# Turning new activations by DMA instead of by TensorE at the stage boundaries of a two-layer encoder

## Chip, cores and metric

The kernel runs on one core of one Trainium2 chip. The metric is the time of one execution in microseconds (us). Five engines work side by side, each through its own list of instructions in order: TensorE (PE, matrix products), VectorE (DVE), ScalarE (ACT), GpSimd (POOL) and SyncE (SP). DMA transfers are started by instructions in an engine's list, run on their own, and report by a semaphore.

## The reference

512 tokens of 1024 values pass two layers of four stages each, every stage ending in a residual and a layer norm.

```python
for i in range(DEPTH):   # 2
    x = layer_norm(ALPHA * x + 0.5 * swiglu(x, ffn_w_in[i, 0], ffn_w_out[i, 0]), ...)   # f
    x = layer_norm(ALPHA * x + token_mix(x, mix_w_in[i], ..., mix_w_out[i]), ...)        # m
    x = layer_norm(ALPHA * x + 0.5 * swiglu(x, ffn_w_in[i, 1], ffn_w_out[i, 1]), ...)   # f
    ple = sigmoid(x @ ple_w_gate[i] + ple_b_gate[i]) * (p[i] @ ple_w_proj[i])           # p
    x = layer_norm(ALPHA * x + ple, ...)

def swiglu(x, w_in, w_out):          # w_in 1024 x 5632, w_out 2816 x 1024
    gate, up = split(x @ w_in, 2, axis=-1)
    return (silu(gate) * up) @ w_out
```

`token_mix` is a projection to heads of stick-breaking attention, of a chunked gated delta rule and of a short convolution, and an output projection. All is float32.

## The kernel before

**Number format.** Every float32 factor of a product is split into a float16 high part and a float16 rest, `hi` and `lo`; `mm3` (L254) makes a product of three float16 products (L256 hi·hi, L257 hi·lo, L258 lo·hi). Weights come in by SP's DMAs as float32 (`raw`, three buffers; `f` for quads) and are split by `split_part`: ACT makes `hi` (L139), DVE makes `lo` (L140).

**Tiles.** Tokens stand in four tiles `t` of 128. `x_tok` holds x in token order, tokens on partitions. A product wants x with the 1024 features on partitions: `xT`, as `hi` and `lo`. At the end of each stage the out projection `out_proj(t)` (PE `po`, DVE adds the residual, L472) and `layer_norm(t)` make new x tile by tile. There are seven boundaries between stages: f to m twice, m to f twice, f to p twice, p to f once. At each, four tiles are turned.

**The turn.** `layer_norm` only notes the tile in `pending`; a later `flush` calls `to_T`: eight 128×128 float32 transpositions on PE into two PSUM banks (L220, `ps_t`), ACT copies `hi` into `xT` (L223), DVE subtracts for `lo` (L224). Flushes stand between the tiles of `out_proj`, in the gate stage (`ple`) and in the mix, and for the last tile in the ffn behind the first projections of the other three tiles.

**The ffn.** Its first two columns of 128 (m = 0, 1) are plain products. Three accumulators (`ahead`: gate m = 0, up m = 0, gate m = 1) are run first over tokens 0 to 383 and then, when the last tile is there, over 384 to 511; the up projection m = 1 follows when a silu (L345) has freed an accumulator. All other columns go in units of two by a scheme of seven products on 2×2 blocks (`begin`, `step`), which needs sums of weight blocks (`load_quad`, L453) and four sums of blocks of x, `xS`: halves of the features of even and odd token tiles combined. Before, they are formed from the PSUM banks (`ts`, L232, L236, L238) and split by `put_sums` (L248, L249). The products of a unit are numbered 0 to 6; those with `sums(n)` read `xS`. The columns are done in four groups, each followed by an `out_proj` over all tiles.

**Order.** The program is recorded stage by stage and a scheduler sets each engine's list; `after(a, b)` adds an order by hand. The buffers of `t2` (six) are shared by most temporaries.

Of the kernel before, what the change touches and what calls it, by code (L numbers as in the profile page):

```python
# [17 lines left out]
P = 128  # L18
D = 1024
# [14 lines left out]
class Block:  # L34
    def __init__(self, ctx, tc, ins, out):
        self.tc, self.nc, self.ins, self.out = tc, tc.nc, ins, out
        nc = self.nc
        pool = lambda name, **k: ctx.enter_context(tc.tile_pool(name=name, **k))
        self.const = pool("const", bufs=1)
        self.act = pool("act", bufs=1)  # L40
        self.rawp = pool("rawp", bufs=3)
        self.w2 = pool("w2", bufs=4)
        self.tmp = pool("tmp", bufs=6)
        self.small = pool("small", bufs=4)
        self.dram = pool("dram", bufs=2, space=bass.MemoryType.DRAM)
        self.psa = pool("psa", bufs=2, space=PSUM)
        self.psb = pool("psb", bufs=3, space=PSUM)
        self.psc = pool("psc", bufs=3, space=PSUM)
        self.pending, self.block_sums, self.put = [], [], 0
        self.constants()  # L50
# [126 lines left out]
    def layer_norm(self, t, y, gb, last=False):  # L177

        nc = self.nc
        g, b = gb  # L180
        st = self.small.tile([P, 2, 6], F32, name="st")
        for h in range(2):
            nc.vector.bn_stats(st[:, h], y[:, h * 512 : (h + 1) * 512])
        mv = self.small.tile([P, 2], F32, name="mv")
        nc.vector.bn_aggr(mv, st.rearrange("p a b -> p (a b)"))
        rs = self.small.tile([P, 2], F32, name="rs")
        nc.vector.tensor_scalar(rs[:, 0:1], mv[:, 1:2], LN_EPS / ALPHA**2, None, op0=ALU.add)
        nc.gpsimd.tensor_tensor(rs[:, 1:2], rs[:, 0:1], self.mhalf[:, 0:1], op=ALU.pow)
        halves = [y[:, h * 512 : (h + 1) * 512] for h in range(2)]
        for h, yh in enumerate(halves):  # L190
            nc.vector.scalar_tensor_tensor(
                yh, yh, mv[:, 0:1], g[:, h * 512 : (h + 1) * 512], op0=ALU.subtract, op1=ALU.mult
            )
        for h, yh in enumerate(halves):
            nc.vector.scalar_tensor_tensor(
                yh, yh, rs[:, 1:2], b[:, h * 512 : (h + 1) * 512], op0=ALU.mult, op1=ALU.add
            )
            if last:
                nc.sync.dma_start(
                    self.out[t * P : (t + 1) * P, h * 512 : (h + 1) * 512], yh  # L200
                )
        if not last:
            self.pending.append((self.xT, t, y, self.next_sums))

# [5 lines left out]

    def to_T(self, xT, t, y, sums):


        nc = self.nc
        banks = []
        for h in range(2):
            ps = self.bank("ps_t", (P, 4, P))
            for k in range(4):
                c = h * 512 + k * P
                nc.tensor.transpose(ps[:, k], y[:, c : c + P], self.ident)  # L220
            hi, lo = (xT[:, q, 4 * h : 4 * h + 4, t * P : (t + 1) * P] for q in range(2))
# [3 lines left out]
            )  # L225
            banks.append(ps)
        if not sums:
            return
        if t % 2 == 0:
            self.even = [self.t2("ts", (P, 4, P)) for _ in range(2)]  # L230
            for b, ps in zip(self.even, banks):
                nc.scalar.activation(b, ps, AF.Copy)  # L232
        else:
            b11, b21 = self.even
            n1, n2 = (self.t2("ts", (P, 4, P)) for _ in range(2))
            nc.vector.tensor_tensor(n1, b11, banks[0], op=ALU.subtract)  # L236
            for t, a, b in ((n2, banks[1], n1), (b11, n2, b11), (b21, n2, b21)):
                nc.vector.scalar_tensor_tensor(t, a, -1.0, b, op0=ALU.mult, op1=ALU.subtract)  # L238
            self.block_sums.append((n1, n2, b11, b21))

    def put_sums(self, xS):

        for ts in self.block_sums:
            a = self.put % 2
            self.put += 1
            for n, t in enumerate(ts):
                hi, lo = (xS[:, q, n, :, a * P : (a + 1) * P] for q in range(2))
                self.nc.scalar.activation(hi, t, AF.Copy)  # L248
                self.nc.vector.tensor_tensor(lo, t, hi, op=ALU.subtract)  # L249
        self.block_sums = []  # L250


    def mm3(self, ps, a, b, first, last, **k):

        nc = self.nc
        nc.tensor.matmul(ps, a[0], b[0], start=first, stop=False, **k)  # L256
        nc.tensor.matmul(ps, a[0], b[1], start=False, stop=False, **k)  # L257
        nc.tensor.matmul(ps, a[1], b[0], start=False, stop=last, **k)  # L258

    def ffn(self, i, f, j, last=False):  # L260
# [7 lines left out]
        with ExitStack() as ctx:  # L268
# [21 lines left out]

            if self.start:
                wg, wu = self.load_start(w_in, xT)
# [3 lines left out]

            def project(ps, w, m, a, b):
                for k in range(KD):
                    self.mm3(
                        ps[:, a:b], [w[:, h, k, m * P : (m + 1) * P] for h in range(2)],  # L300
                        [xT[:, h, k, a:b] for h in range(2)], k == 0, k == KD - 1,
                    )


# [22 lines left out]
            ahead = [(self.acc("pg"), wg, 0), (self.acc("pu"), wu, 0), (self.bank2("pg"), wg, 1)]  # L327
            for args in ahead:
                project(*args, 0, 384)
            self.flush()  # L330
            self.put_sums(xS)
            for args in ahead:
                project(*args, 384, 512)
            for m in range(2):
                if m == 1:
                    self.put_sums(xS)
                ps = []
# [48 lines left out]
            def step(new, old):  # L386

                if old is not None:
                    product(old.A, old.w, 5, sums(3), False, True)
                if new is not None:  # L390
                    product(new.A, new.w, 2, sums(1), False, False)
                    nc.scalar.activation(half(new.sg, 1), new.A, AF.Copy)  # L392
                if old is not None:
# [7 lines left out]
                if new is not None:  # L401
                    C = self.acc("pC")[:, : 2 * P].rearrange("p (a c) -> p a c", a=2)
                    product(C, new.w, 1, quarter(1, 0), True, True)
                    nc.vector.tensor_tensor(half(new.sg, 0), C, half(new.sg, 0), op=ALU.add)
                    product(new.A, new.w, 6, sums(2), False, False)
                    new.up = self.t2("up", (P, 2, P))
                    nc.scalar.activation(new.up, new.A, AF.Copy)  # L407
                    nc.vector.tensor_tensor(new.up, new.B, new.up, op=ALU.add)

            for gi, (m0, m1) in enumerate(groups):  # L410
# [10 lines left out]
                for t in range(NT):  # L421
                    self.out_proj(
                        t, lambda q, m: hT[(m0 + m) // 2][:, q, m % 2], wo, m1 - m0,
                        0.5 * IWS / ALPHA,
                    )
                    self.flush()
                    if gi == len(groups) - 1:
                        self.layer_norm(t, x[:, t], gb, last)

    def load_quad(self, w_in, m):  # L430
# [20 lines left out]
        def rest():  # L451
            for to, a, b in ((6, 0, 4), (4, 4, 5), (2, 0, 4), (3, 1, 2)):
                nc.vector.tensor_tensor(f[:, to], f[:, a], f[:, b], op=ALU.add)  # L453
            split(slice(4, 7), slice(2, 4))
# [3 lines left out]

    def out_proj(self, t, aT, wo, n, scale):

        for h in range(2):
            po = self.acc("po")
            for m in range(n):
                self.mm3(
                    po,
                    [aT(q, m)[:, t * P : (t + 1) * P] for q in range(2)],
                    [wo[m // 2][:, q, m % 2, h * 512 : (h + 1) * 512] for q in range(2)],
                    m == 0,
                    m == n - 1,
                )  # L470
            xs = self.x[:, t, h * 512 : (h + 1) * 512]
            self.nc.vector.scalar_tensor_tensor(xs, po, scale, xs, op0=ALU.mult, op1=ALU.add)  # L472


    def ple(self, i, j, last=False):
        nc, ins, x, xT = self.nc, self.ins, self.x, self.xT
        self.xT = self.act.tile([P, 2, KD, S], F16, name="xT", tag="xT", bufs=2)
        with self.tc.tile_pool(name="ple", bufs=1, reuse_waits="tile") as pool, \
# [12 lines left out]
            for t in range(NT):  # L491
# [9 lines left out]
                if t == 0:  # L501
                    for c in range(2):
# [10 lines left out]
                        )  # L513
                self.flush()
                for h in range(2):
# [43 lines left out]
    def mix_body(self, i, j, last, pool):  # L559
# [42 lines left out]
        for t in range(NT):  # L602
            if t == 3:
                self.flush()
            ts = slice(t * P, (t + 1) * P)
# [503 lines left out]
        for t in range(NT):  # L1109
            self.out_proj(t, lambda q, m: mT[:, q, m], wo, KD, IWS / ALPHA)  # L1110
            self.flush()
            self.layer_norm(t, x[:, t], gb, last)
# [9 lines left out]
    def load_tile(self, xT, t):  # L1122
        self.nc.sync.dma_start(self.x[:, t], self.ins["x"][0, t * P : (t + 1) * P, :])
        self.pending.append((xT, t, self.x[:, t], True))

    def load_start(self, w_in, xT):
# [4 lines left out]
        for c in range(2):  # L1131
            cs = slice(c * P, (c + 1) * P)
            for raw, w, c0 in zip(raws, ws, (0, DFF)):
# [4 lines left out]
                for k in (slice(0, 4), slice(4, 8)):  # L1138
                    parts = self.split_part(w[:, 0, k, cs], w[:, 1, k, cs], raw[:, k, cs])
                    for later, earlier in zip(parts, self.turned):  # L1140
                        self.after(later, earlier)
            if c == 0:
                self.load_tile(xT, NT - 1)
        return ws

@with_exitstack
def encoder_block(ctx: ExitStack, tc: tile.TileContext, ins, out, stages="fmfp", layers=range(DEPTH)):
# [3 lines left out]
    for (i, j, s), following in zip(n, n[1:] + [None]):  # L1151
        last = following is None
        k.next_sums = not last and following[2] == "f"
        if s == "f":
# [27 lines left out]
```

## Time and profile before

| | us |
|---|---|
| median of three runs | 2005.02 (2003.77 to 2005.6) |
| the profiled execution: its time | 2003.89 |
| its span, first to last instruction | 2002.2 |
| TensorE busy | 1951.1 |
| VectorE busy | 1522.9 |
| ScalarE busy | 870.6 |
| GpSimd busy | 69.9 |

The clock granted to TensorE was 0.997 of full speed. A row of the timeline has start, duration, engine, line, operation, out<-in, and in brackets the idle time before it and what ended it. A row of a group has line, engine, operation and shapes, then busy us and mean ns, then idle time before it by releaser. Products on TensorE overlap: a row's duration is longer than the step from one to the next. "PE x <- ACT y: 5.8, 2, 5.2" reads: PE's x waited for ACT's y 5.8 us in all, twice, the longest 5.2. The boundaries of the first layer stand at about 329 to 360 us (f to m), 599 to 637 (m to f), 932 to 963 (f to p) and 976 to 1023 (p to f).

### The profile page before, as it was taken

The numbers are of one execution on the slowest core, as the hardware profiler recorded it, in microseconds if no ns is written. First come the engines' busy times: TensorE is split into PE (matmuls) and PEld (weight loads), VectorE is DVE, ScalarE is ACT, GpSimd is POOL, SyncE is SP. The second block draws the span as 40 slices with busy tenths as digits, with TensorE's granted clock in tenths as the row PEclk, the third lists the DMA queues.
The fourth block names the chain that finished last, engine by engine and source line by source line (L and its number), as shares of the span: only waits on it lengthen the run. The fifth ranks groups of instructions, "written<-read, shape, count | busy, mean of one in ns | idle before, by whom it ended". The sixth has DMA issues, their size and how long they took to land.

```text
span 2002.2 us, 33105 instructions
## 1 busy us (share of the span) xinstructions
PE 1951.1 (97%) x14058; PEld 1271.2 (63%) x14058; DVE 1522.9 (76%) x2347; ACT 870.6 (43%) x1295; POOL 69.9 (3%) x92
## 2 busy tenths in 40 slices
PE   7999999999999999999999999999999999999998
PEld 5677686545555686776467685854455466776853
DVE  7995866775579895958897867667756897967586
ACT  6453442554445353444364444424634364443430
POOL 1000000110000000000000000002000000000000
PEclk9999999999999999999999999999999999999999
DMA  7543320421253533334224333213222524333221
GB/s 216 194 118 106 106 86 1 127 59 38 71 187 95 157 108 106 106 106 142 111 84 128 106 112 92 72 43 90 53 85 70 184 92 141 106 106 85 95 74 43
DMA packets 245359, 205.15 MB, mean 102 GB/s; under 512 B 20846, under 2 KB 225500, under 8 KB 245212
## 3 DMA queue, kind: packets, MB, share of 16 engines
q1 hardware_dynamic: 245212, 203.05, 33.0%
q8 instruction: 110, 1.80, 0.4%
q14 instruction: 37, 0.30, 0.0%
HBM read 200.14 MB, written 2.88 MB: 101 GB/s over the span
## 4 chain that ended last, share of the span: by engine, by line
PE 73%; DVE 15%; ACT 7%; issue 2%; DMA 2%; SPq 1%; POOL 0%; DVEq 0%; ACTq 0%
PE po L258 7%; PE po L256 7%; PE po L257 7%; PE pA L256 6%; PE pA L258 6%; PE pA L257 6%; DVE w L140 3%; PE pB L258 3%; PE pB L257 3%; PE pB L256 3%; DVE wq L140 2%; ACT w L139 2%; ACT wq L139 2%; PE pC L256 1%; PE pC L258 1%
## 5 line engine op out<-in xcount | busy, mean ns | idle before, releaser
L140 DVE SCALAR_TENSOR_TENSOR wq<-f,wq 128x1024 f16<-128x1024 f32 (+1 forms) x240 | 334.2, 1396 | 19.1 <-ACT wq L139 15.9
L139 ACT ACTIVATE wq<-f 128x1024 f16<-128x1024 f32 (+1 forms) x240 | 279.5, 1191 | 126.1 <-PE pB L258 83.2
L139 ACT ACTIVATE w<-raw 128x1024 f16<-128x1024 f32 (+1 forms) x196 | 193.6, 1031 | 264.9 <-PE po L258 226.2
L256 PE MATMUL po<-w,hT 128*128 128x512 f16 x704 | 266.7, 379 | 3.1 <-ACT hT L286 0.9
L256 PE MATMUL pA<-xS,wq 128*128 128x256 f16 x960 | 261.6, 272 | 6.9 <-ACT up L407 5.3
L257 PE MATMUL po<-w,hT 128*128 128x512 f16 x704 | 266.5, 379 | 0.0
L258 PE MATMUL po<-w,hT 128*128 128x512 f16 x704 | 264.3, 379 | 1.9 <-DVE hT L287 1.9
L258 PE MATMUL pA<-xS,wq 128*128 128x256 f16 x960 | 261.6, 273 | 0.0
L257 PE MATMUL pA<-xS,wq 128*128 128x256 f16 x960 | 261.6, 273 | 0.0
L140 DVE SCALAR_TENSOR_TENSOR w<-raw,w 128x1024 f16<-128x1024 f32 (+1 forms) x196 | 229.5, 1194 | 37.3 <-ACT w L139 37.3
L257 PEld LDWEIGHTS <-wq 128*128 128x128 f16 x2240 | 219.1, 98 | 42.0 <-issue 11.9
L453 DVE TENSOR_TENSOR f<-f 128x512 f32<-128x512 f32 x320 | 218.6, 687 | 27.2 <-DMA f<-in_ffn_w_in 22.1
L256 PEld LDWEIGHTS <-wq 128*128 128x128 f16 x2240 | 219.1, 98 | 30.2
L258 PEld LDWEIGHTS <-wq 128*128 128x128 f16 x2240 | 219.1, 98 | 27.3
L472 DVE SCALAR_TENSOR_TENSOR x_tok<-po,x_tok 128x512 f32<-128x512 f32 x144 | 97.6, 686 | 82.3 <-PE po L258 82.1
L395 DVE TENSOR_TENSOR sg<-pB,sg 128x256 f32<-128x256 f32 x80 | 33.7, 422 | 117.6 <-PE pB L258 117.6
L256 PEld LDWEIGHTS <-hT 128*128 128x128 f16 x704 | 68.8, 98 | 84.7 <-ACT hT L286 9.4
L258 PEld LDWEIGHTS <-hT 128*128 128x128 f16 x704 | 68.0, 98 | 84.8 <-DVE hT L287 5.3
L257 PEld LDWEIGHTS <-hT 128*128 128x128 f16 x704 | 68.9, 98 | 76.8 <-issue 1.3
L392 ACT ACTIVATE sg<-pA 128x256 f32<-128x256 f32 x80 | 30.5, 382 | 194.5 <-PE pA L258 194.5
L257 PEld LDWEIGHTS <-w 128*128 128x128 f16 x640 | 62.6, 98 | 67.0 <-issue 19.4
L223 ACT ACTIVATE xT<-ps_t 128x512 f16<-128x512 f32 x64 | 35.4, 594 | 150.6 <-PE ps_t L220 150.4
(290 smaller groups left out, 3851.5 us busy)
## 6 DMA issues: line engine op xcount, KB each, us to landing
f<-in_ffn_w_in SPq DMA_DIRECT2D x160, 512.0 KB, 5.0
raw<-in_ffn_w_out SPq DMA_DIRECT2D x44, 1024.0 KB, 5.2
raw<-in_mix_w_in SPq DMA_DIRECT2D x28, 1024.0 KB, 5.6
raw<-in_mix_w_out SPq DMA_DIRECT2D x8, 1024.0 KB, 4.9
raw<-in_ple_w_gate SPq DMA_DIRECT2D x8, 1024.0 KB, 6.1
raw<-in_ffn_w_in SPq DMA_DIRECT2D x6, 1024.0 KB, 5.1
ln_gb<-in_ln_g SPq DMA_DIRECT2D x8, 512.0 KB, 3.6
ln_gb<-in_ln_b SPq DMA_DIRECT2D x8, 512.0 KB, 4.7
```

The source lines that it names most:

```text
L139: self.nc.scalar.activation(hi, raw, AF.Copy, scale=WS),
L140: self.nc.vector.scalar_tensor_tensor(lo, raw, WS, hi, op0=ALU.mult, op1=ALU.subtract),
L223: nc.scalar.activation(hi, ps, AF.Copy),
L256: nc.tensor.matmul(ps, a[0], b[0], start=first, stop=False, **k)
L257: nc.tensor.matmul(ps, a[0], b[1], start=False, stop=False, **k)
L258: nc.tensor.matmul(ps, a[1], b[0], start=False, stop=last, **k)
L392: nc.scalar.activation(half(new.sg, 1), new.A, AF.Copy)
L395: nc.vector.tensor_tensor(half(old.sg, 1), old.B, half(old.sg, 1), op=ALU.add)
L453: nc.vector.tensor_tensor(f[:, to], f[:, a], f[:, b], op=ALU.add)
L472: self.nc.vector.scalar_tensor_tensor(xs, po, scale, xs, op0=ALU.mult, op1=ALU.add)
```

## The change

1. `flush` and `to_T` stay for the opening alone (32 transpositions). At a boundary `layer_norm` ends with `turn`: in token order ACT copies `hi` and DVE subtracts `lo` into `t2` tiles ("turn"), and ACT starts a transposing DMA for each into `xT`. Tiles 0 to 2 take two DMAs of 128×1024, tile 3 four of 128×512: 70 over seven boundaries.
2. The token sums are formed by DVE from `x_tok`, split in token order and turned by eight DMAs of 128×1024 per ffn: 32. In all 102 transposing DMAs, all started by ACT.
3. `put_sums` is called for tokens 0 to 255 behind the projections of the first 384 tokens, and for the rest behind those of the last 128.
4. In the first unit of a group product 2 runs after the product C (`sixth`); `out_proj` of the first tile of a group runs all but the last column of both halves first (`late`).
5. In the opening the first projections run in a given order, and the last tile's transpositions and some DVE sums are ordered behind others.

```diff
         if not last:
-            self.pending.append((self.xT, t, y, self.next_sums))
+            self.turn(self.xT, t, y)
...
-        if t % 2 == 0:
-            self.even = [self.t2("ts", (P, 4, P)) for _ in range(2)]
-            for b, ps in zip(self.even, banks):
-                nc.scalar.activation(b, ps, AF.Copy)
...
+    def pair_T(self, out, y, n):
+        nc = self.nc
+        hi, lo = (self.t2("turn", (P, n), F16) for _ in range(2))
+        self.turned = (
+            nc.scalar.activation(hi, y, AF.Copy), nc.vector.tensor_tensor(lo, y, hi, op=ALU.subtract)
+        )
+        for q, v in enumerate((hi, lo)):
+            nc.scalar.dma_start_transpose(out(q), v)
+
+    def turn(self, xT, t, y):
+        n = 1024 if t < NT - 1 else 512
+        for c in range(0, D, n):
+            ks = slice(c // P, (c + n) // P)
+            self.pair_T(lambda q: xT[:, q, ks, t * P : (t + 1) * P], y[:, c : c + n], n)
+
+    def put_sums(self, xS, a):
+        nc = self.nc
+        b11, b21, b12, b22 = (self.x[:, 2 * a + t, 512 * h : 512 * h + 512] for t in range(2) for h in range(2))
+        one, two = (self.tmp4.tile([P, 2, 512], F32, name="ts", tag="ts") for _ in range(2))
+        first = nc.vector.tensor_tensor(one[:, 0], b11, b12, op=ALU.subtract)
+        if self.opening:
+            self.after(first, self.turned[1] if a else self.parts[1])
+        for to, p, m in ((one[:, 1], b22, one[:, 0]), (two[:, 0], one[:, 1], b11), (two[:, 1], one[:, 1], b21)):
+            nc.vector.scalar_tensor_tensor(to, p, -1.0, m, op0=ALU.mult, op1=ALU.subtract)
+        for n, ts in ((0, one), (2, two)):
+            self.pair_T(
+                lambda q: xS[:, q, n : n + 2].rearrange("p n k c -> p (n k) c")[:, :, a * P : (a + 1) * P],
+                ts.rearrange("p n c -> p (n c)"), 1024,
+            )
...
-            for args in ahead:
-                project(*args, 0, 384)
-            self.flush()
-            self.put_sums(xS)
+            self.opening = first
+            for n, args in enumerate(ahead):
+                done = project(*args, 0, 384, done if first and n else None)
+                if first and n == 0:
+                    self.behind = done
+                    self.flush()
+                    self.behind = None
+            self.put_sums(xS, 0)
             for args in ahead:
                 project(*args, 384, 512)
+            self.put_sums(xS, 1)
             for m in range(2):
-                if m == 1:
-                    self.put_sums(xS)
...
-                if new is not None:
-                    product(new.A, new.w, 2, sums(1), False, False)
-                    nc.scalar.activation(half(new.sg, 1), new.A, AF.Copy)
+                if new is not None and old is not None:
+                    sixth(new)
...
                     nc.vector.tensor_tensor(half(new.sg, 0), C, half(new.sg, 0), op=ALU.add)
+                    if old is None:
+                        sixth(new)
...
+        if late:
+            for h in range(2):
+                part(h, range(n - 1))
+        for h in range(2):
+            if late:
+                part(h, [n - 1])
```

How ACT's list changes at three places. First the m to f boundary of the first layer. Before (`wq_6279` the first unit's weights, `xS_5948` the sums, `sg` the silus of m = 0 and 1):

```order
L223 ACTIVATE xT_5633<-ps_t_6055 128x4x128
L139 ACTIVATE wq_6279<-f_6276 128x1024
L139 ACTIVATE wq_6279<-f_6276 128x1536
L248 ACTIVATE xS_5948<-ts_6062 128x4x128
L345 ACTIVATE sg_6156<-pg_5973 128x512
L139 ACTIVATE wq_6279<-f_6276 128x1024
L248 ACTIVATE xS_5948<-ts_6063 128x4x128
L248 ACTIVATE xS_5948<-ts_5930 128x4x128
L248 ACTIVATE xS_5948<-ts_5931 128x4x128
L345 ACTIVATE sg_6187<-pg_5975 128x512
```

Now (`turn_6095` and `turn_6096` are hi and lo of sums 0 and 1 of tokens 256 to 511, `turn_6101` and `turn_6102` those of sums 2 and 3, `w_7157` a tile of out weights):

```order
L236 DMA_TRANSPOSE xS_5899<-turn_6012 128x8x128
L233 ACTIVATE turn_6095<-ts_6089 128x1024
L140 ACTIVATE w_7157<-raw_7155 128x1024
L236 DMA_TRANSPOSE xS_5899<-turn_6095 128x8x128
L236 DMA_TRANSPOSE xS_5899<-turn_6096 128x8x128
L233 ACTIVATE turn_6101<-ts_6090 128x1024
L140 ACTIVATE wq_6230<-f_6227 128x1024
L236 DMA_TRANSPOSE xS_5899<-turn_6101 128x8x128
L236 DMA_TRANSPOSE xS_5899<-turn_6102 128x8x128
L362 ACTIVATE sg_6107<-pg_5924 128x512
L362 ACTIVATE sg_6138<-pg_5926 128x512
```

The silus moved behind all transpositions of the sums, and a split of out weights stands ahead of the last four; it waits for PE's last product of the `ahead` accumulators, whose weight buffer it takes over.

Second, the f to m boundary, ACT, before (`sbv` belongs to the mix's v projections, `pv`):

```order
L223 ACTIVATE xT_201<-ps_t_3488 128x4x128
L139 ACTIVATE w_3671<-raw_3669 128x1024
L139 ACTIVATE w_3755<-raw_3753 128x1024 x2
L611 ACTIVATE sbv_3545<-pv_3547 128x256
L611 ACTIVATE sbv_3545<-pv_3574 128x256
L223 ACTIVATE xT_201<-ps_t_3628 128x4x128
L611 ACTIVATE sbv_3545<-pv_3601 128x256
L223 ACTIVATE xT_201<-ps_t_3635 128x4x128
```

Now:

```order
L140 ACTIVATE w_3732<-raw_3730 128x1024 x2
L233 ACTIVATE turn_3486<-x_tok_143 128x512
L236 DMA_TRANSPOSE xT_190<-turn_3486 128x4x128
L233 ACTIVATE turn_3492<-x_tok_143 128x512
L236 DMA_TRANSPOSE xT_190<-turn_3487 128x4x128
L236 DMA_TRANSPOSE xT_190<-turn_3492 128x4x128
L643 ACTIVATE sbv_3536<-pv_3538 128x256
L643 ACTIVATE sbv_3536<-pv_3565 128x256
L140 ACTIVATE w_3920<-raw_3918 128x1024
L236 DMA_TRANSPOSE xT_190<-turn_3493 128x4x128
```

The last transposition, of tile 3's `lo` for features 512 to 1023, came to stand behind the split of a third weight tile, whose load waits for DVE to have split the first (`w_3648`).

Third, ACT in the opening, before:

```order
L139 ACTIVATE w_656<-raw_654 128x1024
L248 ACTIVATE xS_200<-ts_326 128x4x128
L139 ACTIVATE w_693<-raw_691 128x1024
L248 ACTIVATE xS_200<-ts_196 128x4x128
L248 ACTIVATE xS_200<-ts_197 128x4x128
L139 ACTIVATE w_693<-raw_691 128x1024
L345 ACT_TABLE_LOAD
L345 ACTIVATE sg_419<-pg_236 128x512
```

Now:

```order
L236 DMA_TRANSPOSE xS_189<-turn_327 128x8x128
L140 ACTIVATE w_696<-raw_694 128x1024
L233 ACTIVATE turn_410<-ts_404 128x1024
L140 ACTIVATE w_696<-raw_694 128x1024
L236 DMA_TRANSPOSE xS_189<-turn_410 128x8x128
L236 DMA_TRANSPOSE xS_189<-turn_411 128x8x128
L233 ACTIVATE turn_416<-ts_405 128x1024
L140 ACTIVATE wq_545<-f_542 128x1024
L236 DMA_TRANSPOSE xS_189<-turn_416 128x8x128
L236 DMA_TRANSPOSE xS_189<-turn_417 128x8x128
L362 ACT_TABLE_LOAD
L362 ACTIVATE sg_422<-pg_225 128x512
```

The first silu now stands behind all eight transpositions of the opening's sums.

More of the change, by code (lines that the diff above doesn't have):

```diff
@@ L43, in __init__ @@
         self.tmp = pool("tmp", bufs=6)
+        self.tmp4 = pool("tmp4", bufs=2)
         self.small = pool("small", bufs=4)
@@ L48, in __init__ @@
         self.psc = pool("psc", bufs=3, space=PSUM)
-        self.pending, self.block_sums, self.put = [], [], 0
+        self.pending, self.behind = [], None
         self.constants()
@@ L209, in flush, with to_T @@
         self.pending = []
-    def to_T(self, xT, t, y, sums):
+    def to_T(self, xT, t, y):
         nc = self.nc
-        banks = []
         for h in range(2):
@@ L219, in to_T @@
                 c = h * 512 + k * P
-                nc.tensor.transpose(ps[:, k], y[:, c : c + P], self.ident)
+                turn = nc.tensor.transpose(ps[:, k], y[:, c : c + P], self.ident)
+                if self.behind is not None:
+                    self.after(turn, self.behind)
             hi, lo = (xT[:, q, 4 * h : 4 * h + 4, t * P : (t + 1) * P] for q in range(2))
@@ L225, in to_T @@
             )
-            banks.append(ps)
-        if not sums:
-            return
-        if t % 2 == 0:
-            self.even = [self.t2("ts", (P, 4, P)) for _ in range(2)]
-            for b, ps in zip(self.even, banks):
-                nc.scalar.activation(b, ps, AF.Copy)
[L233 to L253, printed above, removed]
-        nc = self.nc
-        nc.tensor.matmul(ps, a[0], b[0], start=first, stop=False, **k)
+    def pair_T(self, out, y, n):
+        nc = self.nc
+        hi, lo = (self.t2("turn", (P, n), F16) for _ in range(2))
[4 more added lines that the diff above has]
+            nc.scalar.dma_start_transpose(out(q), v)
@@ L257, in mm3 @@
+    def mm3(self, ps, a, b, first, last, behind=None, **k):
+        nc = self.nc
+        begun = nc.tensor.matmul(ps, a[0], b[0], start=first, stop=False, **k)
+        if behind is not None:
+            self.after(begun, behind)
         nc.tensor.matmul(ps, a[0], b[1], start=False, stop=False, **k)
-        nc.tensor.matmul(ps, a[1], b[0], start=False, stop=last, **k)
+        return nc.tensor.matmul(ps, a[1], b[0], start=False, stop=last, **k)
     def ffn(self, i, f, j, last=False):
@@ L289, in ffn @@
             self.quads = 0
-            if self.start:
+            first = self.start
+            if first:
                 wg, wu = self.load_start(w_in, xT)
@@ L295, in ffn, with project @@
                 wu = self.load_cols(w_in, DFF, self.w2)
-            def project(ps, w, m, a, b):
+            def project(ps, w, m, a, b, behind=None):
                 for k in range(KD):
-                    self.mm3(
+                    done = self.mm3(
                         ps[:, a:b], [w[:, h, k, m * P : (m + 1) * P] for h in range(2)],
-                        [xT[:, h, k, a:b] for h in range(2)], k == 0, k == KD - 1,
+                        [xT[:, h, k, a:b] for h in range(2)], k == 0, k == KD - 1, behind,
                     )
+                return done
             loads, loaded = [], []
@@ L408, in step, with sixth @@
                     nc.vector.tensor_tensor(new.up, new.B, new.up, op=ALU.add)
+            def sixth(u):
+                product(u.A, u.w, 2, sums(1), False, False)
+                nc.scalar.activation(half(u.sg, 1), u.A, AF.Copy)
             for gi, (m0, m1) in enumerate(groups):
@@ L423, in ffn @@
                         t, lambda q, m: hT[(m0 + m) // 2][:, q, m % 2], wo, m1 - m0,
-                        0.5 * IWS / ALPHA,
+                        0.5 * IWS / ALPHA, late=t == 0,
                     )
-                    self.flush()
                     if gi == len(groups) - 1:
@@ L452, in rest @@
             for to, a, b in ((6, 0, 4), (4, 4, 5), (2, 0, 4), (3, 1, 2)):
-                nc.vector.tensor_tensor(f[:, to], f[:, a], f[:, b], op=ALU.add)
+                total = nc.vector.tensor_tensor(f[:, to], f[:, a], f[:, b], op=ALU.add)
+                if self.opening and self.quads < 4:
+                    self.after(total, self.turned[1])
             split(slice(4, 7), slice(2, 4))
@@ L457, in load_quad, with out_proj, part @@
         return w, rest
[L459 to L463, printed above, removed]
+    def out_proj(self, t, aT, wo, n, scale, late=False):
+        po = [self.acc("po"), self.acc("po")] if late else [None] * 2
+        def part(h, ms):
+            for m in ms:
                 self.mm3(
-                    po,
+                    po[h],
                     [aT(q, m)[:, t * P : (t + 1) * P] for q in range(2)],
@@ L470, in out_proj @@
                 )
+        if late:
[4 more added lines that the diff above has]
+                part(h, [n - 1])
+            else:
+                po[h] = self.acc("po")
+                part(h, range(n))
             xs = self.x[:, t, h * 512 : (h + 1) * 512]
-            self.nc.vector.scalar_tensor_tensor(xs, po, scale, xs, op0=ALU.mult, op1=ALU.add)
+            self.nc.vector.scalar_tensor_tensor(xs, po[h], scale, xs, op0=ALU.mult, op1=ALU.add)
     def ple(self, i, j, last=False):
@@ L513, in ple @@
                         )
-                self.flush()
                 for h in range(2):
@@ L602, in mix_body @@
         for t in range(NT):
-            if t == 3:
-                self.flush()
             ts = slice(t * P, (t + 1) * P)
@@ L1110, in mix_body @@
             self.out_proj(t, lambda q, m: mT[:, q, m], wo, KD, IWS / ALPHA)
-            self.flush()
             self.layer_norm(t, x[:, t], gb, last)
@@ L1123, in load_tile @@
         self.nc.sync.dma_start(self.x[:, t], self.ins["x"][0, t * P : (t + 1) * P, :])
-        self.pending.append((xT, t, self.x[:, t], True))
+        self.pending.append((xT, t, self.x[:, t]))
     def load_start(self, w_in, xT):
@@ L1142, in load_start @@
             if c == 0:
+                self.parts = parts
                 self.load_tile(xT, NT - 1)
@@ L1152, in encoder_block @@
         last = following is None
-        k.next_sums = not last and following[2] == "f"
         if s == "f":
```

## The prediction

> **What bounds the kernel now.** I read the page's busy shares first, then the chain that ended last.
>
> ```profile
> span 2002.2 us, 33105 instructions
> PE 1951.1 (97%) x14058; PEld 1271.2 (63%) x14058; DVE 1522.9 (76%) x2347; ACT 870.6 (43%) x1295; POOL 69.9 (3%) x92
> PE 73%; DVE 15%; ACT 7%; issue 2%; DMA 2%; SPq 1%; POOL 0%; DVEq 0%; ACTq 0%
> ```
>
> TensorE (PE) works 97% of the span, so a microsecond taken from its stream, or a microsecond for which it waits, is a microsecond of the kernel. The profiled execution took 2003.89 us, 1.7 more than its span; the median of the runs shown is 1.1 above it. The sum is made against 2003.9 and 1.1 is added at the end. A change under 0.2% (4 us) could not be told from none.
>
> The waits of PE come next (sum in us, times, longest).
>
> ```profile
> PE pu L256 <- ACT sg L345: 5.8, 2, 5.2
> PE pA L256 <- ACT up L407: 5.3, 11, 1.8
> PE po L258 <- DVE hT L287: 1.9, 2, 0.9
> PE ps_t L220 <- DVE x_tok L195: 1.1, 1, 1.1
> PE po L256 <- ACT hT L286: 0.9, 4, 0.3
> PE pg L256 <- ACT xT L223: 0.8, 2, 0.4
> PE po L256 <- DVE sg L404: 0.7, 1, 0.7
> PE pv L256 <- DVE w L140: 0.5, 2, 0.3
> PE pg L257 <- DVE xT L224: 0.4, 2, 0.2
> ```
>
> Boundary waits are small: 2.8 us together (1.1, 0.8, 0.5, 0.4). The present scheme therefore costs PE its transpositions and little else.
>
> **Removed from PE.** Two answers: the group of the transpositions, and PE's timeline where one flush stands between products of the mix's out projection (start, us, engine, line).
>
> ```profile
> L220 PE MATMUL ps_t<-ident,x_tok x256: 272/273/445, 4.6 to 1951.5; 128*128 128x128 f32 x128
> ...
> 596.64 0.38 PE L258 MATMUL po<-w,mT 128*128 128x512 f16 x1
> ...
> 599.23 0.38 PE L258 MATMUL po<-w,mT 128*128 128x512 f16 x1
> 599.45 1.04 PE L220 MATMUL ps_t<-ident,x_tok 128*128 128x128 f32 x8
> 600.32 0.38 PE L256 MATMUL po<-w,mT 128*128 128x512 f16 x1
> ```
>
> Matmuls overlap, so the duration of 273 ns is not the price. From 596.64 to 599.23 stand twelve steps of a 512-wide product, so one is 0.216. Across the flush the step is 600.32 − 599.23 = 1.09: a flush of eight costs 0.87. Of 256 transpositions 32 belong to the opening and stay; 224 / 8 = 28 flushes go: 28 × 0.87 = **−24.4**. The 2.8 of boundary waits go with them: **−2.8**. By the Trainium skill ("VectorE: DVE Perf Modes", the rules for kernel authors) one should turn 128×128 on TensorE where PSUM will do, and take the DMA's crossbar otherwise; its table gives 390 ns against 1309. This trace has 0.11 us a block on PE's path, which makes the rule stronger here, but neither figure says what the DMA's time costs PE; that hangs on the cover, below.
>
> **Product order and held-back last products** (`sixth`, `late`). They aim at waits of the third fence: up 5.3, hT 1.9 + 0.9, sg 0.7, together 8.8. The opening's 1.8 and the two pairs near 0.9 look movable; the 0.3 ones repeat at groups that hold no spare product. I take a little over half, **−5**; ends 0 and −8.8.
>
> **What a turn costs now.** A tile's turn is an ACT copy, a DVE difference, and two DMAs that ACT issues in its own order. The copies have rows (behind the bar: busy us, mean ns; the page's list of DMAs: KB each, median us to landing; the DMA queue's timeline: start, us); no DMA transposition does.
>
> ```profile
> L139 ACT ACTIVATE w<-raw 128x1024 f16<-128x1024 f32 (+1 forms) x196 | 193.6, 1031 | 264.9 <-PE po L258 226.2
> L140 DVE SCALAR_TENSOR_TENSOR w<-raw,w 128x1024 f16<-128x1024 f32 (+1 forms) x196 | 229.5, 1194 | 37.3 <-ACT w L139 37.3
> ...
> raw<-in_mix_w_in SPq DMA_DIRECT2D x28, 1024.0 KB, 5.6
> out<-x_tok SPq DMA_DIRECT2D x8, 256.0 KB, 2.0
> ...
> 633.86 0.37 SPq L439 DMA_DIRECT2D f<-in_ffn_w_in  x1
> 354.69 9.27 SPq L148 DMA_DIRECT2D raw<-in_mix_w_in  x4
> ```
>
> So 1.03 for the copy, 1.19 for the difference. Landing: the nearest row is the 256 KB store out of the same x tile, 2.0 (the same bytes, also from SBUF); ends 2.0 and 5.6. Issue: 0.37 when the queue is idle, 9.27 / 4 = 2.3 when four large loads stand in it; ACT's queue carries nothing else, so I take 0.4.
>
> **Where PE then waits.** PE keeps its order; each stall is the landing less the work that covers it.
>
> *Mix to ffn, twice.* Rows of DVE and PE at the first such boundary:
>
> ```profile
> 612.18 0.69 DVE L183 BATCH_NORM_STATS2 st<-x_tok 128x6 f32<-128x512 f32 x1
> 617.88 1.41 DVE L195 SCALAR_TENSOR_TENSOR x_tok<-x_tok,rs,ln_gb 128x512 f32<-128x512 f32 x2
> ...
> 623.33 0.32 PE L256 MATMUL pg<-xT,w 128*128 128x384 f16 x1 [0.38 <-ACT xT L223]
> 635.22 0.33 PE L258 MATMUL pg<-xT,w 128*128 128x384 f16 x1
> ...
> 636.94 0.27 PE L256 MATMUL pA<-xT,wq 128*128 128x256 f16 x1
> 637.05 0.27 PE L257 MATMUL pA<-xT,wq 128*128 128x256 f16 x1
> ```
>
> Tile 2: after its out projection DVE runs six half-row steps of 0.6 (residual, statistics, two of the token sums, two weight sums) and the norm's four passes (2.7, twice the L195 row's 1.41 less overlap), 6.3; copy 1.0, difference 1.2, issue 0.4, landing 2.0: 10.9. PE's next out projection covers 48 × 0.216 = 10.4. Stall 0.4. Tile 3 has 12 us of cover (623.33 to 635.22) and needs none. Then ACT's queue: a split of out weights (`w_7157`) waits for PE's last first-projection product; the transpositions of the second token half's sums stand behind it. Split 1.03, two issues 0.8, landing 2.0, less 12 products × 0.11 = 1.3 that PE still has: stall 2.5. Both: 2 × 2.9 = **+5.8**.
>
> *Ffn to mix, twice.* ACT's last transposition (`turn_3493`) now stands behind a split whose load needs a buffer that DVE empties 3.7 after the last out projection (residual and statistics 1.2, two splits of 1.2, a short one). Load 5.6, split 1.0, issue 0.4, landing 2.0: 12.7. PE reads it in the middle of the fourth v projection:
>
> ```profile
> 353.28 0.28 PE L256 MATMUL pv<-wvab,xT 128*128 128x264 f16 x1
> 353.39 0.28 PE L257 MATMUL pv<-wvab,xT 128*128 128x264 f16 x1
> ```
>
> 84 products × 0.112 = 9.4. Stall 3.3; 2 × 3.3 = **+6.6**. The lower end is 0, if the load is early.
>
> *Gate stage to ffn, once.* The last tile's turn ends at 9.7 (DVE: residual, three weight splits, norm) + two half differences 1.3 + issue 0.4 + landing 2.0 = 13.4; cover 12.0 + 0.7. With the same 2.5 at the sums: **+3.2**.
>
> *Ffn to gate stage.* Before, DVE reaches the gate 6.9 after the residual of the last tile, and ACT splits a late load:
>
> ```profile
> 950.69 0.68 DVE L472 SCALAR_TENSOR_TENSOR x_tok<-po,x_tok 128x512 f32<-128x512 f32 x1
> 957.59 0.68 DVE L518 SCALAR_TENSOR_TENSOR gate<-pgate,bg 128x512 f32<-128x512 f32 x1
> ...
> 959.95 2.00 ACT L139 ACTIVATE w<-raw 128x1024 f16<-128x1024 f32 x2 [1.01 <-DMA raw<-in_ffn_w_out]
> ```
>
> Now five halves of weight splits and three turn differences stand ahead of the gate: 13.7 after the out projection, or 17 if the last tile's copy waits behind that late split; PE needs the accumulator that the gate frees at 48 × 0.216 = 10.4. I take **+4** (ends 0 and 6.7). The second time no ffn follows and none of these splits are there: 0.
>
> *Opening.* ACT reaches the first silu 7.3 after the out weights land:
>
> ```profile
> 26.78 1.06 ACT L139 ACTIVATE w<-raw 128x1024 f16<-128x1024 f32 x1 [4.58 <-DMA raw<-in_ffn_w_out]
> 32.77 1.28 ACT L345 ACT_TABLE_LOAD   x1
> 34.06 0.60 ACT L345 ACTIVATE sg<-pg 128x512 f32<-128x512 f32 x1
> ```
>
> The up projection waits for it (5.2, third fence). In the new order eight issues (3.2), three more 1024-wide copies (3.1) and a wait for the DVE sums stand between; I count it through to 41.1 for the silu's start, 7.1 later. PE has 17 products × 0.11 = 1.9 to put there: **+5.2**; ends 0 and 10.
>
> **Sum.** −24.4 − 2.8 − 5 + 5.8 + 6.6 + 3.2 + 4 + 5.2 = −7.4: 1996.5 for such an execution, 1997.6 with the 1.1; **1998**.
>
> **Rivals.**
> 1. *Hidden anyway.* All boundary transpositions land in time and only the opening's 5.2 stays: −24.4 − 2.8 − 5 + 5.2 = −27, 1978. For it: stalls are 0.4 to 3.3, small against covers of 9 to 12, and DVE loses the PSUM sums. Against it: the split ahead of the sums waits for PE itself, whatever lands when. Chance 0.25.
> 2. *ACT's issue time* (the other side). About 28 issues lie on the paths above (8 mix to ffn, 2 ffn to mix, 6 gate to ffn, 4 ffn to gate, 8 opening). Each 0.1 us of issue is 2.8 us; the gain is gone at 0.4 + 7.4 / 28 = 0.66, and at 1.4, inside the 2.3 row, the time is 1997.6 + 28 = 2026. Against it is the 0.37 row. Chance 0.14. The Trainium skill ("DMA: Bandwidth & Descriptors", the table of instruction times in the sequencer) gives earlier generations 262,144 cycles for 8,192 tiles, 32 a tile, which is this rival's mechanism; with tiles of 16 rows by 128 columns a wide turn would be 64 tiles, an estimate of 2,048 cycles; no row here shows such an instruction.
> 3. *Slow landing.* Eight places above hold a landing. At 5.2, about a weight load's, the sum gains 8 × 3.2 = 26: 2023. It decides from 2.0 + 7.4 / 8 = 2.9. Chance 0.07. Against it: the store row. If a turn went block by block at the 1309 ns that the Trainium skill ("VectorE: DVE Perf Modes", the three transpose paths) gives, eight blocks would be an estimate of 10.5 us and the sum would come to 1997.6 + 8 × 8.5 = 2066; no row here shows it.
> 4. *Nothing comes of it*: the norm's chain on DVE, not PE, sets each boundary, and PE waits out what it saved. DVE is 15% of the chain; but after a flush PE's next product mostly waits for nothing. 2003 ± 4. Chance 0.10.
>
> **Numbers.** My sum has 0.44, with its own range 1988 to 2006: three quarters faster by over 0.2%, the rest the same. Faster 0.33 + 0.25 = 0.58; same 0.11 + 0.08 = 0.19; slower 0.14 + 0.07 + 0.02 = 0.23. For eight in ten the range cuts into rival 1's low side and rivals 2 and 3's high one: 1978 to 2016.
>
> **What would show it.** The group of transpositions on PE shrinks from 256 to 32 its stream shrinks by 24 and its waits grow by 17 (24.8 new, 7.8 gone); the issue rows of ACT show 0.4 and the DMA list a landing near 2. PE's waits name DMA xS at three boundaries (2.5 each) and DMA xT at the ffn to mix ones (3.3), the gate's DVE row once (4), and the opening's wait for the silu grows from 5.2 to above 10. The prediction fails if issue or landing is twice what I took, or if those waits are not there.

## The result: slower by 2.3%

The changed kernel takes 2052.31 us (median of 4 runs, 2048.45 to 2055.12) against 2004.63 for the one before on the same chip: ratio 1.0233, 95% interval 1.0220 to 1.0246. The forecast was 1998 with a range of 1978 to 2016. The page of the changed kernel (its profiled execution took 2048.45):

```profile
span 2046.7 us, 32786 instructions
PE 1943.5 (95%) x13834; PEld 1256.2 (61%) x13834; DVE 1526.9 (75%) x2310; ACT 862.3 (42%) x1242; POOL 70.1 (3%) x92
```

PE's transpositions did shrink to the opening's 32:

```profile
L219 PE MATMUL ps_t<-ident,x_tok 128*128 128x128 f32 x32 | 5.7, 339 | 4.8 <-POOL masks L75 4.6 <-DVE xT L225 0.2
```

The span grew by 44.5. Its two parts, from the first two lines here and those of the prediction: PE's idle time went from 2002.2 − 1951.1 = 51.1 to 103.2, **+52.1**; PE's busy time fell by 7.6 where 24.4 of work had left, so the rest took **16.8 longer**. The waits of PE after (sum, times, longest) say where the idle time is:

```profile
PE pA L266 <- ACT wq L140: 13.9, 1, 13.9
PE pv L266 <- ACT sbv L643: 11.6, 2, 5.8
PE pB L266 <- ACT turn L233: 10.5, 2, 6.1
PE pg L269 <- DMA xT<-turn: 6.6, 6, 2.2
PE pgate L266 <- DVE gate L552: 4.7, 2, 4.3
...
PE pB L266 <- DMA xS<-turn: 4.3, 1, 4.3
...
PE pu L266 <- ACT sg L362: 3.0, 1, 3.0
```

The three largest name ScalarE, an engine 42% busy. In the third the name misleads. PE's product reads `xS` and not `turn`; here are ScalarE's rows and PE's product at the first of the two places:

```profile
657.62 1.04 ACT L140 ACTIVATE w<-raw 128x1024 f16<-128x1024 f32 x1
657.75 3.80 ACTq L236 DMA_TRANSPOSE xS<-turn  x2
661.60 1.06 ACT L233 ACTIVATE turn<-ts 128x1024 f16<-128x1024 f32 x1 [2.93 <-DVE f L474]
```

```profile
662.76 0.29 PE L266 MATMUL pB<-xS,wq 128*128 128x256 f16 x1 [4.43 <-ACT turn L233]
```

The transposition issued at 657.75 landed 4.9 us later, at 662.6, which is also when the copy of 661.60 ended. So this wait is for a landing, like the row "DMA xS" of 4.3; it is ScalarE's only in that the transposition was issued late. With SyncE issuing (below) all three waits at the sums name the DMA.

What occupies ScalarE is not in its busy time, since issuing is not counted. The answer for the line that issues has it (ns, min/median/max):

```profile
L236 ACTq DMA_TRANSPOSE xT<-turn x70: 1204/1249/4131, 338.4 to 1992.1; - x70
L236 ACTq DMA_TRANSPOSE xS<-turn x32: 1248/1313/3530, 26.8 to 1672.9; - x32
```

And the list of DMAs (median us to landing):

```profile
xT<-turn ACTq DMA_TRANSPOSE x70, 3.2
xS<-turn ACTq DMA_TRANSPOSE x32, 4.9
```

An issue takes 1.2 us or more, not 0.4, and the durations of all 102 add to 151 us. The opening shows how that delays what PE waits for (ScalarE's timeline; ACTq rows are issues):

```profile
26.79 1.06 ACT L140 ACTIVATE w<-raw 128x1024 f16<-128x1024 f32 x1 [3.83 <-DMA raw<-in_ffn_w_out]
26.80 5.02 ACTq L236 DMA_TRANSPOSE xS<-turn  x2
31.87 1.06 ACT L233 ACTIVATE turn<-ts 128x1024 f16<-128x1024 f32 x1 [4.02 <-issue]
...
42.04 1.04 ACT L140 ACTIVATE wq<-f 128x1024 f16<-128x1024 f32 x1
42.17 4.87 ACTq L236 DMA_TRANSPOSE xS<-turn  x2
47.07 1.28 ACT L362 ACT_TABLE_LOAD   x1 [3.99 <-issue]
48.37 1.08 ACT L362 ACTIVATE sg<-pg 128x512 f32<-128x512 f32 x2
```

The out weights land at the same 26.8 as before. The wait of 13.9 is for the weight split `wq` at 42.04, which stands behind six of the eight transpositions. Behind the last two stands the silu: it starts at 48.4 instead of 34.1, and PE waits another 3.0 for it.

To place the 44.5, I took the same landmarks on PE's timeline in both kernels (starts and ends of out projections and of the attention products) and noted how much the changed one gained or lost between them. Two later experiments stand beside it.

| Stretch (us lost against before) | changed | sums not turned | started by SyncE |
|---|---|---|---|
| opening, to the end of the second group | 11.4 | 1.4 | 2.4 |
| ffn to mix, first | 3.1 | 2.8 | 0.4 |
| mix to ffn, first | 7.5 | 0.5 | 4.8 |
| ffn to gate stage and through it, first | 0.3 | −0.1 | 1.2 |
| gate stage to ffn | 9.1 | 0.7 | 4.6 |
| ffn to mix, second | 2.5 | 3.3 | 0.9 |
| mix to ffn, second | 7.9 | 0.3 | 4.0 |
| last gate stage | 1.0 | 4.2 | 4.3 |

A flush removal is already in these: a boundary that lost 7.5 lost 11 and was given 3.5. The four places with token sums hold 35.9 of the 44.

The slower busy time is a clock matter. Behind the opening's waits PE's products of 512 columns step by 0.43 us, and from 51.9 on by 0.21 (PE's timeline):

```profile
50.25 0.63 PE L266 MATMUL pu<-xT,w 128*128 128x512 f16 x1
50.67 0.63 PE L269 MATMUL pu<-xT,w 128*128 128x512 f16 x1
...
51.93 0.38 PE L269 MATMUL pu<-xT,w 128*128 128x512 f16 x1
52.14 0.38 PE L270 MATMUL pu<-xT,w 128*128 128x512 f16 x1
```

The kernel before has such products too, behind its own wait of 5.2 in the opening. From 40 to 1990 us its clock stays whole. In the changed kernel it falls to half in nine more stretches of 3.4 or 6.8 us. The first row is of the kernel before, the second of the changed one behind its first wait for `sbv` (stretch, its length, busy us with counts for PE, PEld, DVE, ACT and POOL, then granted clock, DMA share, GB/s):

```profile
40.00:1990.00 1950.00, 1921.21 (x13853) 1252.39 (x13852) 1486.16 (x2285) 842.32 (x1253) 63.71 (x61) 1.00 0.33 100
366.00:372.60 6.60, 5.48 (x25) 3.53 (x24) 2.94 (x3) 2.55 (x4) 0.00 (x0) 0.50 0.84 210
```

In the nine stretches PE is busy for 32.2 us at a granted clock of 0.50. At twice the step half of that is lost: about 16 us, an estimate that accounts for the 16.8.

### The profile page after: what moved, and what is told of

Its sections match the earlier page's. It is cut to its first block, busy times and chain, and to the rows that moved or that the text cites. A ratio compares the mean times of both kernels' runs of the same rounds, so it can differ in the third digit from the quotient of the medians.

```text
span 2046.7 us, 32786 instructions
## 1 busy us (share of the span) xinstructions
PE 1943.5 (95%) x13834; PEld 1256.2 (61%) x13834; DVE 1526.9 (75%) x2310; ACT 862.3 (42%) x1242; POOL 70.1 (3%) x92
## 5 line engine op out<-in xcount | busy, mean ns | idle before, releaser
L269 PEld LDWEIGHTS <-w 128*128 128x128 f16 x640 | 63.7, 100 | 69.8 <-issue 20.0
L270 PEld LDWEIGHTS <-w 128*128 128x128 f16 x640 | 63.6, 99 | 64.6 <-issue 10.4
```

Source lines behind the costliest of these rows:

```text
L270: return nc.tensor.matmul(ps, a[1], b[0], start=False, stop=last, **k)
```

## Experiments

Two theories were told apart. Theory I: the time to issue a transposing DMA, spent in the in-order list of the engine that starts it, makes what stands behind it late. Theory L: the landing is late, or the transfers hold up the weight loads.

**Another engine issues.**

```diff
-            nc.scalar.dma_start_transpose(out(q), v)
+            nc.sync.dma_start_transpose(out(q), v)
```

> All 102 transposing DMAs are started by SyncE instead of ScalarE; nothing else is edited. Theory I (issue): each transposition holds the list of the engine that starts it for 1.2 us or more, whatever its size, 151 us of ScalarE in all, and the silus, weight splits and copies behind it come late; with ScalarE free, the 13.9 us wait of the opening falls below 8 and the time to 2015-2035. The transpositions still follow one another on SyncE, so DMA waits for xT and xS stay. Theory L (landing): the transpositions land late or hold up the weight loads, whoever starts them; time within 4 us of 2052, or above it.

2029.57 us, ratio 1.0119 (1.0104 to 1.0134): 22.7 less than the changed kernel. The issue costs the same on SyncE (the issuing line, first fence), and the landings are alike (3.2 and 4.7 in the list of DMAs). The other two fences are from ScalarE's timeline and from PE's waits:

```profile
L236 SPq DMA_TRANSPOSE xT<-turn x70: 1189/1236/1877, 329.4 to 1969.7; - x70
L236 SPq DMA_TRANSPOSE xS<-turn x32: 1237/1288/4860, 22.8 to 1655.1; - x32
```

```profile
39.50 1.08 ACT L362 ACTIVATE sg<-pg 128x512 f32<-128x512 f32 x2
```

```profile
PE pB L266 <- DMA xS<-turn: 12.4, 3, 5.4
PE pA L266 <- ACT wq L140: 8.2, 3, 7.6
```

ScalarE's first silu comes at 39.5, 8.9 sooner, and the opening's longest wait, for the split `wq`, falls from 13.9 to 7.6. So about half of the loss was ScalarE's list. The transpositions still go one after another, now on SyncE, and PE waits for their end at the sums (12.4).

**More issues, the same bytes.**

```diff
-        n = 1024 if t < NT - 1 else 512
+        n = 512
```

> Every tile is turned in four pieces of 128x512 as tile 3 is, so 42 more transposing DMAs with the same bytes. Theory I: 42 x 1.25 = 52 us more of ScalarE's list, most of it where PE waits; 2070-2095. Theory L: half the bytes each, so each lands no later; 2045-2056.

2066.73, ratio 1.0305 (1.0287 to 1.0322): 14.4 more. That is below the forecast of theory I, and far outside that of L; of 52 us of extra issuing a quarter reached the path. A piece of half the size is issued hardly faster (median 1225 ns against 1249) though it lands sooner (2.6 against 3.2):

```profile
L236 ACTq DMA_TRANSPOSE xT<-turn x112: 1203/1225/2163, 337.8 to 2004.7; - x112
```

**Fewer issues.**

```diff
-        n = 1024 if t < NT - 1 else 512
+        n = 1024
```

> The changed kernel with tile 3 turned by two DMAs of 128x1024 like the others: 14 transpositions fewer, the same bytes. Theory I: 17 us less in ScalarE's list, 2040-2049. Theory L: the last tile lands later, 2052-2060.

2044.13, ratio 1.0191 (1.0174 to 1.0208): 8.2 less than the changed kernel, as theory I has it. Cutting the last tile into smaller pieces was itself a loss.

**The token sums not turned.**

```diff
...
+        if plain:
+            r = lambda v: v.rearrange("p (k c) -> p k c", c=P)
+            nc.scalar.activation(out(0), r(y), AF.Copy)
+            nc.vector.tensor_tensor(out(1), r(y), out(0), op=ALU.subtract)
+            return
...
-                ts.rearrange("p n c -> p (n c)"), 1024,
+                ts.rearrange("p n c -> p (n c)"), 1024, plain=True,
```

> Leaves out the turn of the token sums: ScalarE and VectorE write the two halves of each sum to xS in token order, so the products read values that are not turned; 32 DMAs fewer, the copies as many. Theory I: the opening and the three boundaries that lead to an ffn lose most of their excess (36 us together), 2015-2028. Theory L, with the landing of xT to blame at every boundary: 2040 or more.

2017.83, ratio 1.0057 (1.0042 to 1.0072): 34.5 less than the changed kernel. The table shows the loss all but gone at the four places with sums (35.9 to 2.9); at the ffn to mix boundaries it stays, and the last gate stage lost 3 more, for a reason that was not looked for. Late weight loads, the other half of theory L, are not what this removed: in the list of DMAs `raw<-in_ffn_w_out` lands after 6.2 us here, 6.0 in the changed kernel and 5.2 before, `raw<-in_ple_w_gate` after 7.8, 8.3 and 6.1.

**Issue alone.** To part issue from landing, small transpositions were put back that nobody reads, in the kernel whose sums are not turned (the edit is against that one).

```diff
+            for q in range(2):
+                spare = self.small.tile([P, 1, P], F16, name="spare", bufs=5)
+                nc.scalar.dma_start_transpose(spare, out(q)[:, 0])
             return
```

> e1_plain_sums (token sums written without a turn, 2018) with 32 small transposing DMAs of 128x128 on ScalarE put back at the places of the sums' own, into tiles that nothing reads. An eighth of the bytes, and PE never waits for their landing. Theory I (a fixed issue time of about 1.2 us per transposition in ScalarE's list): 38 us more in that list, 2026-2045. Theory L (their landing, or their bytes): 2014-2022.

2027.86, ratio 1.0112 (1.0097 to 1.0127): 10.0 more than without them. One of 128×128 holds the list for 1152 ns, with an eighth of the bytes:

```profile
L237 ACTq DMA_TRANSPOSE spare<-xS x32: 1109/1152/1610, 26.7 to 1645.9; - x32
```

So issue alone costs 10 of the sums' 34.5. The rest would be what PE pays when it also needs what is issued last: its wait then ends behind every issue ahead of it, plus the landing. That part is argued; no run here has the landing without the issue. Two caveats make 10 a low figure. The scheduler put the first silu ahead of three of the opening's eight transpositions, so the opening, 10 of the 34.5, was hardly tried (it lost 1.6 here); at the two mix to ffn boundaries issue alone brought back 2.9 and 3.4 of about 7. And the sums' own issues were longer, 1.31 in the median and up to 3.5.

**The accumulators at ffn to mix.** There the changed kernel waits 5.8 us for `sbv`, a small copy that frees an accumulator:

```profile
362.12 0.63 ACT L233 ACTIVATE turn<-x_tok 128x512 f16<-128x512 f32 x1 [1.71 <-DVE x_tok L196]
362.78 1.21 ACTq L236 DMA_TRANSPOSE xT<-turn  x1
364.09 0.63 ACT L233 ACTIVATE turn<-x_tok 128x512 f16<-128x512 f32 x1 [1.34 <-DVE ab L642]
364.11 2.53 ACTq L236 DMA_TRANSPOSE xT<-turn  x2
366.69 0.38 ACT L643 ACTIVATE sbv<-pv 128x256 f32<-128x256 f32 x1 [1.97 <-DVE w L141]
```

```diff
-            pv = self.acc("pv")
+            pv = self.acc("pv") if t < 2 else self.bank("pv")
```

> The changed kernel with one edit: in the mix the v products of tiles 2 and 3 take PSUM banks of another pool, so they no longer wait for the copies sbv of tiles 0 and 1, which stand on ScalarE behind the copies and transpositions of tile 3. If that queue is the cause at the ffn to mix boundaries (5.8 us waited twice, and 0.8 of slow clock each), 6 to 13 us less than the changed kernel: 2039-2046. If tile 3's last transposition is the cause, as predicted (3.3 us twice), PE waits for it instead and the time stays within 3 us of 2052.

2043.10, ratio 1.0202 (1.0184 to 1.0219): 9.2 less than the changed kernel. The `sbv` row is gone from PE's waits, and what it had covered shows, the wait for tile 3's transposition:

```profile
PE pv L266 <- DMA xT<-turn: 4.7, 2, 2.5
...
PE pv L270 <- DMA xT<-turn: 3.5, 2, 2.1
```

**The clock.** TensorE was given useless products in the opening's wait.

```diff
-                project(*args, 384, 512)
+                done = project(*args, 384, 512)
             self.put_sums(xS, 1)
+            if first:
+                spare = self.bank("spare")
+                for _ in range(52):
+                    filler = nc.tensor.matmul(spare, wg[:, 0, 0, 0:P], xT[:, 0, 0], start=True, stop=True)
+                    self.after(filler, done)
+                    done = filler
```

> The changed kernel with 52 extra products of 512 columns on TensorE (11.2 us at full clock, result unused) in the long wait of the opening. If idle time itself lowers TensorE's clock, the products behind the wait run at full step (0.22 us instead of 0.43) and the granted clock of 40-60 us reads 1.0; the time is 1 to 3 us less. If the clock falls for another reason (the transpositions, DMA load), the slow products stay.

2057.52, ratio 1.0267 (1.0253 to 1.0281): 5 more, so the time was forecast wrongly; the scheduler put the up projection ahead of the pA products, and the wait that was left, 10.3 us for the silu, had nothing in it. The windows still decide on the clock. The changed kernel first, then the one with the filler (columns as above):

```profile
30.00:40.00 10.00, 0.00 (x0) 0.00 (x0) 7.01 (x8) 4.96 (x5) 0.00 (x0) 0.57 1.07 199
40.00:50.00 10.00, 2.42 (x8) 0.96 (x9) 5.82 (x8) 4.92 (x6) 0.00 (x0) 0.50 1.04 225
```

```profile
30.00:40.00 10.00, 9.04 (x42) 3.99 (x41) 6.85 (x8) 4.95 (x5) 0.00 (x0) 1.00 1.06 201
40.00:50.00 10.00, 0.67 (x2) 0.26 (x2) 5.75 (x8) 4.60 (x6) 0.00 (x0) 0.58 1.01 224
```

From 30 to 40 us both have the same transfers (1.07 and 1.06, 199 and 201 GB/s) and the same work on ScalarE; with PE idle the clock reads 0.57, with PE busy 1.00, and it falls where the filled kernel idles. In this stretch idle time lowers the clock, not the transfers. The Trainium skill ("TensorE: Matmul & The Clock Gate", Part 1, What's actually happening) states this as a gate that halves the rate after an idle window of about 3.4 us and releases it after as long a busy one. The same page of the Trainium skill (Part 1, Wait — 56ns, not 53.3ns?) has starts 426.7 and 215.7 ns apart at 512 columns. The trace agrees, with 0.43 and 0.22 and with stretches of 3.4 or 6.8 us.

**The order edits alone.** The kernel before with `sixth` and `late`, no DMA turn.

> The kernel before with only the later product 2 in the first unit of a group and the held-back last products of the first tile; no transposition by DMA. As predicted: about 5 us less than before, 1996-2002. Rival: those waits only move to the next product, within 2 us of before.

2003.13, ratio 0.9992 (0.9982 to 1.0002): no difference that can be told. The waits moved:

```profile
PE pA L256 <- ACT sg L413: 3.9, 6, 1.0
PE ps_t L220 <- DVE x_tok L195: 2.9, 3, 1.1
PE po L258 <- DVE hT L287: 2.7, 10, 0.5
...
PE pA L256 <- ACT up L408: 2.3, 8, 0.3
```

The up wait fell from 5.3 to 2.3, a wait for sg of 3.9 took its place, and the wait for hT at L258, which the edits were to shorten, grew from 1.9 to 2.7.

**What is left to gain.** DMA turns only at the two ffn to mix boundaries, v products on other banks, and the order edits; once with ScalarE issuing, once with SyncE.

```diff
...
-            self.pending.append((self.xT, t, y, self.next_sums))
+            if self.by_dma:      # the next stage is the mix
+                self.turn(self.xT, t, y)
+            else:
+                self.pending.append((self.xT, t, y, self.next_sums))
...
```

> The kernel before with the two order edits, the ffn to mix boundaries alone turned by DMA (started by ScalarE) and the two v products on other banks; no token sums by DMA. If transpositions cost only what they hold up, 8 removed flushes of 0.87 give 7 us less a rest of waits: 1995-2001. If the issue time of 1.25 us is paid here too, 2001-2008.

> The same with SyncE starting the 20 transpositions. With ScalarE's list free of them 1995-2000; if SyncE's weight loads behind them come late, above 2003.

2003.15, ratio 0.9995 (0.9986 to 1.0004), and 2003.09, ratio 0.9993 (0.9984 to 1.0002). Neither beats the kernel before by more than can be told. In the first, PE waits 2.4 and 1.3 us for the last tile's transposition at the first such boundary, against 3.5 that the removed flushes give. No version here is better than before.

## Why the prediction was wrong, step by step

1. *Removed from PE, −24.4:* right in kind. 224 transpositions are gone; PE's busy time shows only 7.6 of it, because 16.8 of slow products stand against it. The 2.8 of boundary waits held 0.5 that is a weight split's (`pv`), and left out 1.2 for `ts` (PE `ps_t` behind ACT L232).
2. *Issue, 0.4:* the step that failed first. It measures 1.25, on ScalarE and SyncE alike. My bounds came from plain loads, 0.37 and "2.3"; the second was a misreading, as the 9.27 us row of four issues held waits between them (see the fence behind this list). No row of the kernel before bears on the issue of a transposition, and I took the mildest. The second rival named the mechanism and its break-even of 0.66; at 1.25 its own count of 28 issues gives 1997.6 + 28 × 0.85 = 2021. That is a count and not a measurement; what the runs show is that taking the issues off ScalarE gives back 22.7.
3. *Landing, 2.0:* measured 3.2 (xT) and 4.9 (sums), beyond the 2.9 of the third rival. At five xT places and three sums places that is 5 × 1.2 + 3 × 2.9 = 15, hence 2036.
4. *Mix to ffn and gate to ffn, 2.5 for the sums:* the place was right, the cause not. I had put the wait on one weight split in front of the last transpositions. In the trace that split (657.62, in the fence on the third wait) has no idle time before it. Rather, all of ScalarE's list from the last tile's copy on is late: 12 transpositions, which at the first such boundary took 1.2 to 1.3 each for `xT` and 2.7 to 3.8 a pair for `xS`, and then a landing of 4.9. PE waited 4.3 to 6.1 there. The last tile, which I had put at no wait at mix to ffn, held PE for up to 2.2 (`pg` behind DMA `xT`). Tile 2's stall, 10.9 less 10.4, should have read 0.5; that is 0.2 in the sum.
5. *Ffn to mix, 3.3:* the wrong wait. I followed the transposition that PE reads and missed the copies that free its accumulators, which came to stand behind the last tile's copies and issues, and so behind its norm. They held PE for 5.8 each time. The wait that I had named is real but smaller, and was hidden: with the other banks PE waits 8.2 over the two boundaries, 4.7 for the last tile's first `hi` and 3.5 for its last `lo`, the one that I had named.
6. *Ffn to gate, +4:* right; PE waited 4.3 for the gate, once. The last gate stage was put at no cost and lost 1.0 against before, so it gave back the 3.5 of its flushes and more.
7. *Opening, +5.2:* the silu was put 7.1 later and came 14.3 later; the pairs of issues there took 2.7 to 5.0 while the weight loads were under way. I missed that the second weight split of the first unit stood among them: of the 17 products that I gave PE for the wait, 12 could run, and the other five waited 13.9 for it.
8. *Product order, −5:* nothing that can be told; the waits moved on.
9. *Not in the sum at all:* the clock behind the waits, 16.8.

The issues of step 2, of the kernel before, with their waits left out (ns, min/median/max; 26 of the 28):

```profile
L148 SPq DMA_DIRECT2D raw<-in_mix_w_in x26: 367/378/394, 262.9 to 1487.6; - x26
```

Steps 2 to 5, 8 and 9 put back together come near the measured time: 2036, plus 5 for ffn to mix, plus 3 to 5 for the order edits, plus 16.8, is about 2062 against 2052. How much of the slow clock is already inside the larger waits was not parted.

## What to carry to other kernels

Price an issue on the engine that issues it, and count every issue ahead of whatever PE will wait for; an engine 42% busy by its instructions can still be the bound through its queue. Before work is moved into an in-order list, list what stands behind it there, small copies that free accumulators above all, not only the data that the consumer reads. A new wait of some microseconds on TensorE can cost more than itself, because the products behind it start at half speed.

## What was not expected of the hardware

A transposing DMA between SBUF tiles holds the issuing list 1.15 us for 128×128, 1.2 for 128×512 and 1.25 to 1.31 for 128×1024: nearly a fixed price, about three times that of a plain load (0.37). These are medians: issued in pairs beside weight loads (DMA share 1.0 and more) two took up to 5.0, and a single one up to 4.1. Products behind waits of some 4 us or more, and at three places behind shorter ones (at most 2.2), ran at twice the step, 0.43 for 0.216, at a granted clock of 0.50.
